# A LoRA kernel on one core: the first two stores are released by seven turned tiles of the fourth group

## The chip, the cores and the metric

The kernel runs on one core of one Trainium2 chip. The metric is the device time of one execution in microseconds (us). The kernel before was run three times: 123.61 us median, 123.61 to 123.78. The profile is of one execution that took 123.76 us by the same clock; its span, from the first instruction to the last, is 121.9 us, and 1.8 us lie around the span. The engines are TensorE (PE, with its weight loads as PEld), VectorE (DVE), ScalarE (ACT), GpSimd (POOL) and SyncE (SP), which here only issues transfers. The transfers are carried by the core's 16 DMA engines.

## The reference

```python
def setup_inputs():
    batch, seq, d_model, r = 16, 512, 768, 16
    return {
        "x": np.random.randn(batch, seq, d_model).astype(np.float32),
        "A": np.random.randn(d_model, r).astype(np.float32) * 0.1,
        "B": np.random.randn(r, d_model).astype(np.float32) * 0.1,
        "scale": 0.5,
    }

def reference(x, A, B, scale):
    lora = np.matmul(np.matmul(x, A), B)
    return (x + scale * lora).astype(np.float32)
```

x has 8192 rows of 768 float32 numbers, 25.2 MB. It is read once and a result of the same size is written once. A and B are 48 KB each. The arithmetic is one thin product with A (768 to 16), one with B (16 to 768) and an addition.

## The kernel before

**Tiles and groups.** A tile is 128 rows of x. The 64 tiles form eight groups of 8 (`GROUP`), numbered 0 to 7 in the code, so that the "fourth group" is group 3. All of x passes through one buffer in SBUF, `x_all`, with room for 48 tiles; the last 16 tiles use the place of the first 16 again. The result is added into the same place and stored from there. Row p of a partition holds neighbouring rows of x, so one partition's share of a transfer is one piece of 6, 18, 24 or 48 KB: such a piece is one DMA packet, each DMA engine carries the pieces of 8 of the 128 partitions, and after its 8 pieces of a transfer it writes 4 bytes that count as its part of the transfer's completion.

**One group's way.** ScalarE and GpSimd each cast 4 of the 8 tiles to half precision (`narrowed`, L186 to L196, into `xn`). VectorE turns the 8 tiles in blocks of 32 by 32 (`turned`, L248 to L250, `xn` to `xt`), viewed as 32-bit words, so that one tile is 384 elements a partition. TensorE multiplies with A in 24 matmuls (`projected`, L278 to L291). ScalarE scales the result into `y_bd` with four instructions (L238). TensorE multiplies with B, two tiles at a time (`raised`, L293 to L310): p from 0 to 3 is the pair, and each pair ends with an increment of `s_lora`. VectorE adds each pair to x (`summed(g, p)`, L252 to L259).

**Order on VectorE.** The loop at L265 to L271 is: for group g, wait for the product with A of group g (`s_y`, L267) and for both casts of group g+1 (`s_narrow`, L268), turn group g+1 in one instruction (L269), then add the four pairs of group g. So the fourth group is turned at g = 2, between the additions of group 1 and those of group 2.

**Order on TensorE.** In the loop at L324: pairs 0 and 1 of a group, then the wait for the next group's turn (`s_turned`), half of its product with A, pairs 2 and 3, the other half.

**Order on SyncE.** This engine issues all transfers, in the order in which they stand, and a wait holds back all that stands behind it:

- loads 0 to 5, which are tiles 0 to 47 (load 5 is the 16 tiles of groups 4 and 5, 6144 KB), without a wait among loads 2 to 5 (L160);
- `summed(0)` and `summed(1)`: wait until groups 0 and 1 are added;
- the wait of the change, L169: `s_lora` at 2 * 4 + 2 = 10, that is, TensorE has finished pairs 0 and 1 of group 2;
- store 0 (group 0) and store 1 (group 1), 3072 KB each;
- wait until store 0 is complete, then load 6 (group 6, in the place of group 0); wait until store 1 is complete, then load 7 (group 7);
- `summed(2)`, then the wait on `s_raise` at 6 (L181: TensorE has begun pair 0 of group 5), then store 2 (groups 2 and 3, 6144 KB);
- stores 3 and 4 (6144 KB each), each when VectorE has added its groups.

The loads and stores named here are those of the lists `LOADS` (L106) and `STORES` (L128).

Of the kernel before, what the change touches and what calls it, by code (L numbers as in the profile page):

```python
# [16 lines left out]
GROUP = 8  # L17
# [11 lines left out]
def kernel(  # L29
# [20 lines left out]
    PAIRS = GROUP // 2  # L50
# [32 lines left out]
    def sem(name):  # L83
        sems.append(nc.alloc_semaphore(name))
        return sems[-1]
# [10 lines left out]
    def memory(t2, i, s, n):  # L96
        S = PARTS[i]
        return t2[ds(parts[i], S * P), :].rearrange("(p s) d -> p s d", s=S)[:, ds(s, n), :]

    def held(i, s, n):  # L100
        return tiles(where.index((i, s)), n)

    def tiles(t, n):
        return x_all[:, ds(t % ROOM, n), :]
# [14 lines left out]
    s_first, s_narrow, s_turned, s_taken = sem("s_first"), sem("s_narrow"), sem("s_turned"), sem("s_taken")  # L119
    s_y, s_spread, s_lora = sem("s_y"), sem("s_spread"), sem("s_lora")  # L120

    s_free = [sem(f"s_free{p}") for p in range(PAIRS)]
    s_out0, s_out1, s_raise = sem("s_out0"), sem("s_out1"), sem("s_raise")

    s_sum, s_out = sem("s_sum"), sem("s_out")

# [8 lines left out]
    def on_sync(e):  # L135
        def load(k):
            ld = LOADS[k]
            e.dma_start(out=held(*ld), in_=memory(x2, *ld)).then_inc(s_load[k], 16)  # L138

        def summed(k):  # L140
            e.wait_ge(s_sum, k + 1)
            if STORED[k] + 1 < NG:

                e.sem_inc(s_free[PAIRS - 1], 1)

        def store(k, done):
            st = STORES[k]
            e.dma_start(out=memory(out2, *st), in_=held(*st)).then_inc(done, 16)

        load(0)  # L150
        load(1)
        e.wait_ge(s_ready, 1)
        blocks = A.rearrange("(c e) r -> c (e r)", e=64)
        for c in range(SETS):
            e.dma_start(
                out=a_rows[c : SET * SET : SET, :], in_=blocks[ds(c * SET, SET), :]
            ).then_inc(s_a, 16)
        e.wait_ge(s_brows, 1)
        e.dma_start(out=b_rows[0 : R * APART : APART, :], in_=B).then_inc(s_b, 16)
        for k in range(2, len(LOADS) - 2):  # L160
            load(k)

        for p in range(2, PAIRS):
            e.sem_inc(s_free[p], 1)
        summed(0)
        summed(1)


        e.wait_ge(s_lora, 2 * PAIRS + 2)  # L169
        store(0, s_out0)  # L170
        store(1, s_out1)
        e.wait_ge(s_out0, 16)
        load(len(LOADS) - 2)
        e.wait_ge(s_out1, 16)
        load(len(LOADS) - 1)
        for k in range(2, len(STORES)):
            summed(k)
            if k == 2:


                e.wait_ge(s_raise, 6)  # L181
            store(k, s_out)
# [58 lines left out]
    def on_vector(e):  # L241
        e.wait_ge(s_a, SETS * 16 + 1)
        e.transpose(  # L243
            out=a_t[0:Q].rearrange("i k r c -> i (k r) c"),
            in_=a_rows[0:Q].rearrange("c (i k r) -> c (k r) i", k=2, r=R),
        ).then_inc(s_ready, 1)

        def turned(first, n):  # L248
            ts = [v[:, ds(first, n), :].bitcast(fp32) for v in (xt, xn)]
            return e.transpose(out=ts[0], in_=ts[1])  # L250

        def summed(g, p):  # L252
            xs = tiles(g * GROUP + 2 * p, 2)
            e.wait_ge(s_lora, g * PAIRS + p + 1)
            ins = e.tensor_tensor(out=xs, in0=xs, in1=lora[p % 2], op=mybir.AluOpType.add)  # L255
            if p + 1 == PAIRS and g in STORED:
                ins.then_inc(s_sum, 1)
            elif g + 1 < NG or p + 2 < PAIRS:
                ins.then_inc(s_free[p], 1)  # L259

        for h in range(2):
            e.wait_ge(s_first, h + 1)
            ins = turned(h * SUB, SUB)
        ins.then_inc(s_turned, 1)
        for g in range(NG):  # L265
            if g + 1 < NG:
                e.wait_ge(s_y, g + 1)  # L267
                e.wait_ge(s_narrow, 2 * (g + 1))  # L268
                turned(0, GROUP).then_inc(s_turned, 1)  # L269
            for p in range(PAIRS):  # L270
                summed(g, p)  # L271

    def on_tensor(e):
# [58 lines left out]
        for p in range(PAIRS):  # L332
            raised(p)

    on_sync(nc.sync)
    on_gpsimd(nc.gpsimd)
    on_scalar(nc.scalar)
    on_vector(nc.vector)
    on_tensor(nc.tensor)

# [43 lines left out]
```

## Time and profile before

| what | value |
|---|---|
| median of three runs | 123.61 us (123.61 to 123.78) |
| profiled execution | 123.76 us, span 121.9 us |
| DMA queue, share of 16 engines over the span | 96.8%, 50.43 MB |
| DVE busy | 81.7 us (67%) |
| PE busy | 50.5 us (41%) |
| ACT busy, POOL busy | 37.4 us, 28.4 us |
| stores 0 and 1 issued from | 43.92 us |
| load 6 issued | 55.30 us |
| load 7 issued | 62.70 us |
| store 2 issued | 74.87 us |
| store 4 issued | 101.04 us |

All points in time are counted from the start of the span. A chain of waits names, for each stretch, the work that the next step waited for; a stretch that is called DMA runs from the issue of a transfer to its completion, so it holds both the time in which the transfer waits behind others and the time in which its bytes move. The trace also keeps, for each DMA packet, its start, its duration and its size; the 4-byte packets mark the moment at which one DMA engine has finished its part of one transfer.

### The profile page before, as it was taken

Reading aid. Unit: us, or ns where it says so; the run is one execution under the profiler, and the core shown is the slowest. Engines: PE = TensorE matmul, PEld = TensorE weight load, DVE = VectorE, ACT = ScalarE, POOL = GpSimd, SP = SyncE. Lnnn points to the kernel's source line nnn. Section 1 sums busy time; section 2 is a strip of 40 time slices with the busy share of each in tenths; the row PEclk is TensorE's granted clock in tenths of the full one; section 3 lists DMA queues with packets and bytes.
Section 4 is the critical chain, followed back from the end, with each engine's and each line's share of the span. In section 5 each row is a group of like instructions: output and inputs, shape, how many; then the busy total and the mean of one; then the engine's idle time right before and its main releaser. Section 6 shows DMA issues by size and latency. Waiting matters only on the chain.

```text
span 121.9 us, 885 instructions
## 1 busy us (share of the span) xinstructions
PE 50.5 (41%) x322; PEld 29.3 (24%) x322; DVE 81.7 (67%) x42; ACT 37.4 (31%) x43; POOL 28.4 (23%) x24
## 2 busy tenths in 40 slices
PE   0000239487457457647756714774674320000000
PEld 0000026244233233424424402442442110000000
DVE  0003850799999999999999959999995991000000
ACT  4003929444426402917230093643004000000000
POOL 7732638044026002607100090630000000000000
PEclk9999999999999999999999999999999985555555
DMA  3999999999997996999989999998998999899890
GB/s 67 421 429 429 443 443 403 451 435 419 476 516 339 435 516 298 460 403 443 443 363 460 427 427 468 451 484 387 419 500 387 403 516 403 371 516 419 355 516 0
DMA packets 1928, 50.43 MB, mean 414 GB/s; under 512 B 236, under 2 KB 236, under 8 KB 392
## 3 DMA queue, kind: packets, MB, share of 16 engines
q1 hardware_dynamic: 1928, 50.43, 96.8%
HBM read 25.26 MB, written 25.17 MB: 414 GB/s over the span
## 4 chain that ended last, share of the span: by engine, by line
DVE 33%; DMA 29%; PE 9%; ACT 6%; POOL 2%; issue 2%; SPq 0%; DVEq 0%
DVE x_sb L255 21%; DMA x_sb<-in_x_dram 20%; DVE xt L250 12%; DMA out_dram<-x_sb 9%; PE ps_yt L281 6%; ACT xn L194 3%; PE lora_ps L302 3%; ACT y_bd L238 2%; POOL xn L194 2%; SPq L138 0%; SPq L379 0%; DVEq L268 0%; SPq L133 0%
## 5 line engine op out<-in xcount | busy, mean ns | idle before, releaser
L255 DVE TENSOR_TENSOR x_sb<-x_sb,lora_ps 128x1536 f32<-128x1536 f32 x32 | 53.7, 1735 | 1.4 <-PE lora_ps L302 1.4
L302 PE MATMUL lora_ps<-b_mm,y_bd 128*128 128x512 f16 (+1 forms) x128 | 25.1, 328 | 23.7 <-ACT y_bd L238 15.3
L194 ACT CAST xn<-x_sb 128x3072 f16<-128x3072 f32 (+1 forms) x9 | 23.4, 2609 | 37.2 <-DMA x_sb<-in_x_dram 28.0
L250 DVE STREAM_TRANSPOSE xt<-xn 128x3072 f32<-128x3072 f32 (+1 forms) x9 | 27.0, 3005 | 6.7 <-PE ps_yt L281 4.9
L194 POOL CAST xn<-x_sb 128x3072 f16<-128x3072 f32 (+1 forms) x8 | 20.7, 2588 | 45.3 <-DMA x_sb<-in_x_dram 28.6
L281 PE MATMUL ps_yt<-xt,w_bd 128*128 128x256 f16 x192 | 25.7, 285 | 11.9 <-DVE xt L250 11.9
L281 PEld LDWEIGHTS ps_yt<-xt,w_bd 128*128 128x128 f16 x192 | 18.7, 100 | 19.6 <-issue 15.0
L302 PEld LDWEIGHTS lora_ps<-b_mm,y_bd 128*128 128x128 f16 x128 | 10.5, 97 | 36.8 <-ACT y_bd L238 17.5
L238 ACT ACTIVATE y_bd<-ps_yt 32x256 f16<-32x256 f32 x32 | 12.0, 374 | 17.7 <-PE ps_yt L281 17.4
L243 DVE STREAM_TRANSPOSE a_t<-a_rows 32x1024 f32<-32x1024 f32 x1 | 1.9, 1945 | 11.2 <-DMA a_rows<-in_A_dram 11.2
L315 PE MATMUL lora_ps<-b_half,pick 128*128 128x512 f16 (+1 forms) x2 | 0.8, 500 | 12.5 <-POOL b_half L212 12.5
L315 PEld LDWEIGHTS lora_ps<-b_half,pick 128*128 128x128 f16 x2 | 0.1, 105 | 12.5 <-issue 12.5
L220 POOL COPY w_bd<-w_one 32x384 f16<-32x384 f16 x4 | 2.0, 501 | 0.2
L212 POOL CAST b_half<-b_rows 128x768 f16<-128x768 f32 x1 | 0.8, 830 | 4.5 <-DMA b_rows<-in_B_dram 4.5
L194 ACT ACT_TABLE_LOAD x1 | 1.3, 1283 | 0.9 <-SPq L133 0.9
L202 POOL MEMSET w_bd<- 128x1536 f32 x1 | 1.4, 1372 | 0.0
L199 POOL MEMSET a_rows<- 32x1024 f32 x1 | 0.9, 941 | 0.5 <-SPq L133 0.5
L214 POOL CAST w_one<-a_t 32x384 f16<-32x384 f32 x1 | 0.8, 847 | 0.9 <-DVE a_t L243 0.9
L231 ACT CAST b_mm<-lora_ps 128x768 f16<-128x768 f32 x1 | 0.8, 798 | 0.0
L200 POOL MEMSET b_rows<- 128x768 f32 x1 | 0.7, 727 | 0.0
L203 POOL MEMSET y_bd<- 128x512 f32 x1 | 0.5, 514 | 0.0
L205 POOL TENSOR_SCALAR_AFFINE_SELECT pick<-pick 128x128 f16<-128x128 f16 x1 | 0.3, 300 | 0.0
(5 smaller groups left out, 0.6 us busy)
## 6 DMA issues: line engine op xcount, KB each, us to landing
out_dram<-x_sb SPq DMA_DIRECT2D x3, 6144.0 KB, 20.0
x_sb<-in_x_dram SPq DMA_DIRECT2D x5, 3072.0 KB, 14.8
x_sb<-in_x_dram SPq DMA_DIRECT2D x1, 6144.0 KB, 41.9
out_dram<-x_sb SPq DMA_DIRECT2D x2, 3072.0 KB, 14.9
x_sb<-in_x_dram SPq DMA_DIRECT2D x1, 2304.0 KB, 9.7
x_sb<-in_x_dram SPq DMA_DIRECT2D x1, 768.0 KB, 4.5
a_rows<-in_A_dram SPq DMA_DIRECT2D x3, 16.0 KB
b_rows<-in_B_dram SPq DMA_DIRECT2D x1, 48.0 KB, 7.4
```

The lines of the kernel that those rows point to most:

```text
L194: ins = copy(out=xn[:, ds(first, n), :], in_=tiles(t, n))
L199: e.memset(a_rows[0:Q], 0.0).then_inc(s_ready, 1)
L202: e.memset(w_bd.rearrange("p c k m -> p (c k m)").bitcast(fp32), 0.0)
L212: e.tensor_copy(out=b_half, in_=b_rows).then_inc(s_bh, 1)
L220: e.tensor_copy(out=w_bd[ds(b * Q, Q), :, :, ds(b * Q, R)], in_=w_one).then_inc(s_w, 1)
L238: last = e.mul(out=y_bd[q, :, q], in_=y_ps[q, :, :], mul=sc)
L243: e.transpose(out=a_t[0:Q].rearrange("i k r c -> i (k r) c"), in_=a_rows[0:Q].rearrange("c (i k r) -> c (k r) i", k=2, r=R),).then_inc(s_r ...
L250: return e.transpose(out=ts[0], in_=ts[1])
L255: ins = e.tensor_tensor(out=xs, in0=xs, in1=lora[p % 2], op=mybir.AluOpType.add)
L281: mm = e.matmul(y_ps, w_bd[:, c, k, :], xv[:, :, c, :, k], start=(m == 0), stop=(m == MMS - 1),)
L302: mms.append(e.matmul(t[:, k, ds(n0, w)], y_bd[:, 2 * p + k, :], b_mm[:, ds(n0, w)], start=True, stop=True,))
L315: last = e.matmul(lora[0][:, 0, ds(n0, w)], pick.rearrange("p b r -> p (b r)"), b_half[:, ds(n0, w)], start=True, stop=True,)
```

## The change

SyncE no longer waits for TensorE's tenth pair. It waits for a new semaphore, `s_most`, which VectorE raises when it has turned seven of the eight tiles of group 3. For that, the turn of group 3 becomes two instructions, one of 7 tiles and one of 1; the second carries the increment of `s_turned` for which TensorE waits. The other groups' turns stay one instruction of 8 tiles (the first group has two of 4, before and after).

```diff
@@ -121,6 +121,7 @@
     s_free = [sem(f"s_free{p}") for p in range(PAIRS)]
     s_out0, s_out1, s_raise = sem("s_out0"), sem("s_out1"), sem("s_raise")
+    s_most = sem("s_most")
@@ -166,7 +167,7 @@
         summed(1)
-        e.wait_ge(s_lora, 2 * PAIRS + 2)
+        e.wait_ge(s_most, 1)
         store(0, s_out0)
         store(1, s_out1)
         e.wait_ge(s_out0, 16)
@@ -266,7 +267,11 @@
             if g + 1 < NG:
                 e.wait_ge(s_y, g + 1)
                 e.wait_ge(s_narrow, 2 * (g + 1))
-                turned(0, GROUP).then_inc(s_turned, 1)
+                if g == 2:
+                    turned(0, GROUP - 1).then_inc(s_most, 1)
+                    turned(GROUP - 1, 1).then_inc(s_turned, 1)
+                else:
+                    turned(0, GROUP).then_inc(s_turned, 1)
             for p in range(PAIRS):
                 summed(g, p)
```

## The prediction

> **What bounds the kernel now.** I read the DMA part of the page first, then the shares by stage, then the chain of waits around the stores, and last VectorE's and SyncE's instructions in order of time.
>
> The page's queue line, and a table of stages with, after the clock, the DMA share and GB/s:
>
> ```profile
> q1 hardware_dynamic: 1928, 50.43, 96.8%
> ...
> 32.00:46.00 14.00, 8.08 (x54) 4.85 (x55) 14.00 (x7) 4.69 (x7) 2.75 (x1) 1.00 1.04 446
> 46.00:62.00 16.00, 9.76 (x68) 5.78 (x65) 16.00 (x10) 8.30 (x10) 5.50 (x2) 1.00 0.97 410
> 62.00:76.00 14.00, 7.60 (x48) 4.16 (x48) 12.69 (x6) 4.45 (x6) 2.75 (x1) 1.00 0.99 427
> 76.00:90.00 14.00, 8.64 (x59) 5.19 (x60) 14.00 (x9) 4.25 (x5) 2.75 (x1) 1.00 1.05 453
> ```
>
> A packet is booked in the stage where it starts, so a share can pass 1; what is to be seen is that no stage has a hole. The 16 engines move bytes from 2 us to the end: 50.43 MB in (120.6 - 2.0) us is 425 GB/s. The transfers are the bound, and compute matters only where it lets the queue run empty.
>
> The chain of waits seems to say otherwise, since it goes through the very instruction that is moved:
>
> ```profile
> 42.42 1.49 PE lora_ps L302 x8
> 43.91 0.02 issue
> 43.92 11.36 DMA out_dram<-x_sb
> 55.28 0.02 issue
> 55.30 14.76 DMA x_sb<-in_x_dram
> 70.06 0.05 issue
> 70.11 2.76 POOL xn L194
> ```
>
> Store 0 takes 11.36 us from issue to completion, but its 3.15 MB need 7.4 us at 427 GB/s. The other 4 us are waiting behind load 5. The packet records show this: the engines finish load 5 between 46.45 and 47.67, and on each the first packet of store 0 starts within 3 ns of that. Likewise load 6: 14.76 us, 7.4 of them behind store 1. So a transfer ends when the queue gets to it, and its issue may move as long as it still comes before its turn.
>
> **The change part by part.**
>
> ```profile
> 40.17 1.74 DVE L255 TENSOR_TENSOR x_sb<-x_sb,lora_ps 128x1536 f32<-128x1536 f32 x1
> 41.84 3.36 DVE L250 STREAM_TRANSPOSE xt<-xn 128x3072 f32<-128x3072 f32 x1
> 45.12 6.71 DVE L255 TENSOR_TENSOR x_sb<-x_sb,lora_ps 128x1536 f32<-128x1536 f32 x4
> ...
> 43.92 0.82 SPq L148 DMA_DIRECT2D out_dram<-x_sb  x2
> ...
> L250 DVE STREAM_TRANSPOSE xt<-xn 128x3072 f32<-128x3072 f32 x7 | 23.5, 3363 | 6.3 <-PE ps_yt L281 4.9 <-POOL xn L194 1.3
> L250 DVE STREAM_TRANSPOSE xt<-xn 128x1536 f32<-128x1536 f32 x2 | 3.5, 1751 | 0.4 <-ACT xn L194 0.4
> ```
>
> *When the stores go out.* A turn of 8 tiles takes 3363 ns, one of 4 takes 1751: (3363 - 1751) / 4 = 403 ns a tile and 1751 - 4 * 403 = 139 ns an instruction. Seven tiles: 139 + 7 * 403 = 2960 ns. The turn starts at 41.84, when the additions of group 1 leave VectorE; both casts of group 3 ended by 38.7. So `s_most` rises at 44.80 and SyncE issues at about 44.83 (it took 0.03 us after TensorE's pair before). That is 0.91 us **later** than 43.92, not earlier. The two earlier waits on SyncE, for groups 0 and 1, are met by 41.9 in both kernels.
>
> *What stands behind that wait.* On SyncE: stores 0 and 1, loads 6 and 7, and everything after. Store 1's issue moves to 45.25; its turn comes at 53.8. The first engine is free at 46.45, so store 0's lead shrinks from 2.52 to 1.62 us. Is that enough? The trace has two rows for the time from an issue to packets. Store 2 is issued at 74.87; the first engine leaves load 7 at 76.02 and goes on without a hole, so 1.15 us suffice. The first load, into an empty queue, is issued at 0.97; its first packet starts at 1.99 and the others' by 2.65, 1.0 to 1.7 us, with the start of the program in it. I take the nearer row, a transfer joining a running queue: 1.15 is under 1.62, cost 0. From the far row, the last engine could starve by 0.1 us.
>
> *Loads 6 and 7.* They are issued when stores 0 and 1 are complete (54.94 and 62.21 in the packets, 55.30 and 62.70 at SyncE), and their turns come at 61.5 and 68.7: leads of 6 us. Since the stores end when they did, these do not move. If store 0 did end later by up to 6 us, load 6 would still join the queue in time, but every byte behind a hole is late by the hole.
>
> *VectorE.* One more instruction. Alone it is 139 ns; the rows above show the next VectorE instruction starting 0.08 us before the last has ended (41.84 + 3.36 = 45.20 against 45.12), so the net is between 0.06 and 0.14 us; I take 0.10. TensorE's product with A of group 3, group 2's additions and all of groups 3 to 5 move by that. It ends here:
>
> ```profile
> 70.11 2.75 POOL L194 CAST xn<-x_sb 128x3072 f16<-128x3072 f32 x1 [11.66 <-DMA x_sb<-in_x_dram]
> 72.86 1.53 ACT L238 ACTIVATE y_bd<-ps_yt 32x256 f16<-32x256 f32 x4
> 72.97 3.38 DVE L250 STREAM_TRANSPOSE xt<-xn 128x3072 f32<-128x3072 f32 x1 [1.31 <-POOL xn L194]
> ```
>
> VectorE waits 1.31 us for the cast of load 6, which swallows the 0.10. Store 2 waits for ScalarE's scaling at 72.86, which stands behind ScalarE's own cast of load 6, so its lead of 1.15 us is untouched. Were the cover gone, 0.10 us would shorten that lead. Store 4 is issued at 101.04 and its turn comes at 105.0. So this costs 0. The Trainium skill, "VectorE: DVE Perf Modes", section on the TRN2 errata, gives a measured fixed term of about 150 cycles at 0.96 GHz per instruction, some 0.16 us, where this trace has 0.14; either is under 1.31.
>
> *The seam from load 5 to store 0.* One thing can still change. An undisturbed 48 KB packet takes 1.815 us. Of load 5's last ones, four (started 44.98 to 45.41) took 1.946, 1.880, 2.281 and 2.254: a mean of 0.065 us over the 16 engines. At the seam from store 1 to load 6 nine 24 KB packets took 1.1 to 1.7 us instead of 0.912: 0.27 us an engine. The seam from load 7 to store 2, whose store joined just 1.15 us ahead, has no stretched packet. No row shows what a lead of 1.62 us gives. Bounds: all stays (0), or the 0.065 goes and with it what follows. I take the nearer, at most 0.065 gained.
>
> **Sum.** Later stores 0, VectorE 0 (0.10 under 1.31), seam -0.065: the profiled 123.76 becomes 123.70. It lies 0.15 above the median of 123.61; carried over, **123.55 us**. A measurement of this kernel can tell about 0.2%, 0.25 us, from no change.
>
> **The rivals.**
>
> *Faster by the seam (0.32).* If stretched packets come from a store queued well ahead of its turn, the shorter lead removes them, and engines that leave load 5 within 0.8 us of one another (as they left load 4, 31.92 to 32.69) instead of 1.2 may also cross the next seam more cleanly. In full: 0.065 + 0.27 = 0.34 off the mean finish of 120.02, and the last engine 0.24 behind the mean instead of 0.54. The end moves from 120.56 to 119.92: 0.64 less, 123.0. Half of that: 123.3. For it: the clean seam at 76. Against it: the next seam's load has a lead of 6 us in either kernel.
>
> *Slower by a late store (0.13).* If the queue needs a lead over 1.62 us, each engine idles for the missing part and everything behind it is late: 0.25 us at a lead of 1.87; the full 0.91, 124.5, if a lead of 2.52 was just enough. For it: the chain of waits, and 1.7 us for the last engine of the first load. Against it: 1.15 us sufficed at store 2. The Trainium skill speaks for this side: "DMA: Bandwidth & Descriptors", in its rules for kernel authors, says to issue a DMA early so that its fixed cost overlaps. This trace bears that out only as far as the lead of 1.15 us.
>
> *Slower by a worse seam (0.11).* The stagger of the engines changes and the stretched packets fall on the last engine instead: one more of 0.45 us there gives 124.05. Nothing in the trace says which engine they hit.
>
> *That the change does not release as it says* is excluded: `s_most` rises once, and nothing else holds these stores after 41.9.
>
> **How the numbers follow.** No measurable change has 0.44, faster 0.32, slower 0.13 + 0.11 = 0.24. The likeliest alone: 123.4 to 123.8. The range takes in the seam's full gain at 123.0, and on the other side the worse seam and a late store by half its price: 123.0 to 124.15, with about 0.15 outside.
>
> **What would show it.** Stores 0 and 1 issued at 44.8 instead of 43.9; store 0's time to landing 10.4 instead of 11.4 us; load 6 still issued at 55.3; VectorE's wait for GpSimd's cast 1.2 instead of 1.3 us; turns of about 2960 and 540 ns. I am wrong if a DMA engine shows a hole near 46.5, if load 6 goes out later than 55.6, or if the seams near 46 and 61.5 look different.

## The result, and the profile after

The changed kernel took 124.15 us in the median of 7 runs (123.54 to 124.42), beside 123.71 us (123.46 to 123.96) for the kernel before. The ratio is 1.0039, with a 95% interval of 1.0022 to 1.0055: slower by about 0.44 us.

Inside the span nothing is slower. The profiled execution of the change took 124.27 us with a span of 121.9 us; the one before took 123.76 us with the same 121.9 us. The half microsecond lies around the span: 2.4 us instead of 1.8.

First the part that the prediction was about. The chain of waits of the changed kernel around the stores:

```profile
42.01 2.90 DVE xt L251
44.90 0.02 issue
44.92 10.45 DMA out_dram<-x_sb
55.37 0.02 issue
55.38 14.60 DMA x_sb<-in_x_dram
69.98 0.05 issue
70.04 2.76 POOL xn L195
```

The first two stores go out at 44.92 us, one microsecond later than before, and store 0 is complete when it was before, 55.37 against 55.28: its time to completion shrank by 0.9 us because it spends less time behind load 5. Load 6 starts and lands as before (70.06 before, 69.98 now).

The stages of the changed kernel, with clock, DMA share and GB/s at the end of each line, have no hole either:

```profile
32.00:46.00 14.00, 7.93 (x53) 4.72 (x54) 14.00 (x9) 4.79 (x7) 2.75 (x1) 1.00 1.04 451
46.00:62.00 16.00, 9.93 (x69) 5.92 (x67) 16.00 (x10) 8.15 (x10) 5.50 (x2) 1.00 0.97 415
62.00:76.00 14.00, 7.55 (x48) 4.16 (x48) 12.93 (x6) 4.62 (x6) 2.75 (x1) 1.00 1.00 428
76.00:90.00 14.00, 8.73 (x60) 5.25 (x61) 14.00 (x9) 4.26 (x5) 2.75 (x1) 1.00 1.03 446
```

VectorE's turns by shape, with their mean duration, and the idle time before them:

```profile
L251 DVE STREAM_TRANSPOSE xt<-xn 128x3072 f32<-128x3072 f32 x6 | 20.2, 3370 | 5.9 <-PE ps_yt L286 4.8 <-POOL xn L195 1.1
...
L251 DVE STREAM_TRANSPOSE xt<-xn 128x2688 f32<-128x2688 f32 x1 | 3.0, 2966 | 0.0
...
L251 DVE STREAM_TRANSPOSE xt<-xn 128x384 f32<-128x384 f32 x1 | 0.5, 541 | 0.0
```

The pieces take 2966 and 541 ns, and the wait for GpSimd's cast of load 6 shrinks from 1.3 to 1.1 us: the cover holds. In the packet records the end of store 4's last packet moves from 120.56 to 120.48 us.

What is new stands behind the span. This is the list of DMA queues of the changed kernel in the stretch from 120 to 126 us (kind of queue: packets, MB, share):

```profile
q14 instruction: 1, 0.01, 0.5%
q1 hardware_dynamic: 4, 0.00, 0.0%
```

and the same stretch of the kernel before:

```profile
q1 hardware_dynamic: 6, 0.00, 0.1%
```

The packet records put that one instruction packet at 124.00 us, 2.1 us after the last instruction of the span: 8192 bytes, 0.51 us long. By the kind of its queue it carries instructions, not data; for which engine, the records don't say. In the profiled execution of the kernel before, the last instruction packet stands 0.07 us ahead of the span. The last instruction of the span has ended by then; what an execution still does in its last two microseconds is not in the profile.

From here on, "time around the span" is a run's time less its span; each run lists both, the span to 0.1 us, so one such difference is good to 0.05 us. It is 1.94 to 2.54 us in the seven runs of the change, median 2.42; all 107 runs of the kernel before beside the experiments lie between 1.76 and 1.86, median 1.81.

### The profile page after: what moved, and what is told of

Its sections match the earlier page's. It is cut to its first block, busy times and chain, and to the rows that moved or that the text cites. A ratio compares the mean times of both kernels' runs of the same rounds, so it can differ in the third digit from the quotient of the medians.

```text
span 121.9 us, 886 instructions
## 1 busy us (share of the span) xinstructions
PE 50.3 (41%) x322; PEld 29.3 (24%) x322; DVE 81.8 (67%) x43; ACT 37.5 (31%) x43; POOL 28.4 (23%) x24
## 4 chain that ended last, share of the span: by engine, by line
DVE 38%; DMA 29%; PE 6%; ACT 5%; POOL 2%; issue 2%; SPq 0%; DVEq 0%
DVE x_sb L256 23%; DMA x_sb<-in_x_dram 20%; DVE xt L251 15%; DMA out_dram<-x_sb 9%; PE ps_yt L286 5%; ACT xn L195 3%; POOL xn L195 2%; PE lora_ps L307 1%; ACT y_bd L239 1%; SPq L139 0%; SPq L384 0%; DVEq L269 0%; SPq L134 0%
## 5 line engine op out<-in xcount | busy, mean ns | idle before, releaser
L251 DVE STREAM_TRANSPOSE xt<-xn 128x3072 f32<-128x3072 f32 (+3 forms) x10 | 27.2, 2723 | 6.1 <-PE ps_yt L286 4.8
```

## The experiments

Instructions are counted below in the built program, the list that the build makes of the kernel for each engine: 61 on VectorE before, 62 with the change.

Theory A: the added VectorE instruction lengthens that engine's program so that one more piece has to be fetched at the end. Theory B: the late stores cost something. Theory C: the added semaphore does, by one more to clear. Theory D: the cut turn itself does.

**Late stores alone.** No cut, no semaphore.

```diff
-        e.wait_ge(s_lora, 2 * PAIRS + 2)
+        e.wait_ge(s_taken, 4)
```

> The turn of group 3 stays one instruction and no semaphore is added; stores 0 and 1 wait for the second matmul of group 3's product with A (the semaphore s_taken at 4) instead of TensorE's tenth pair. They should be issued near 45.5 us, 1.6 us later than before and 0.7 later than in the change, 0.95 us ahead of their turn. If the loss of the change comes from late stores: slower than the kernel before by at least the 0.44 us of the change (124.15 or more). If the loss comes from what was added to the programs (one VectorE instruction, one semaphore): no loss, 123.7 within 0.2. The span before is 121.9, the rest 1.8 us; a lead under 1.15 us may also open a hole of up to 0.2 us in the queue, which then shows in the packets near 46.5.

Measured: 124.67 us against 123.59, ratio 1.008 (1.0067 to 1.0093). By its time alone that is the costly late store of the expectation. But this loss is inside the span, 122.9 us, and the time around it is 1.81 us. The stores went out not at 45.5 but at 46.38 us, since in this execution VectorE's turn started 0.6 us later and the semaphore came after TensorE's second matmul had ended. The chain of waits of this kernel:

```profile
45.97 0.40 PE ps_yt L281 x2
46.37 0.02 issue
46.38 8.72 DMA out_dram<-x_sb
55.11 0.02 issue
55.12 15.56 DMA x_sb<-in_x_dram
```

The engines left load 5 from 46.64 us on, 0.26 us after the issue, and the first packets of store 0 started at 47.24 to 47.38, 0.86 to 1.00 us after it. That is the time from an issue to its packets, and the queue stood empty for 0.27 us an engine. So a late store does cost when its lead is shorter than that time, about 1 us here; in the change it had 1.8 us in the profiled execution (issued 44.92, first engine free at 46.72). This run therefore doesn't test the change's own release. The larger part of this run's loss came later. Load 6 now takes 15.56 us from issue to landing instead of 14.76. With the engines restarted together, within 0.15 us of one another, they all met the step from store 1 to load 6 at the same moment, and 27 packets there were stretched, 0.80 us an engine against 0.27 before. That the common restart is the reason is read from this one profile and was not tested. The expectation named the hole in the queue, but neither the issue at 46.38 nor the loss at this step.

**The cut alone.** The turn of group 3 in 7 tiles and 1, the stores as before, no semaphore.

```diff
-                turned(0, GROUP).then_inc(s_turned, 1)
+                if g == 2:
+                    turned(0, GROUP - 1)
+                    turned(GROUP - 1, 1).then_inc(s_turned, 1)
+                else:
+                    turned(0, GROUP).then_inc(s_turned, 1)
```

> The turn of group 3 is two instructions, of 7 tiles and 1, and the stores wait for TensorE's tenth pair as before; no semaphore is added. If the added VectorE instruction costs outside the span: 124.1, with the span at 121.7 to 121.9 and 2.3 us or more around it. If late stores or the semaphore cost: 123.7, with 1.8 us around the span.

Measured: 124.23 us, ratio 1.0044 (1.0032 to 1.0057), the whole loss of the change without its late stores. Span 121.6 to 122.0; around it 1.91 to 2.50, median 2.38; an 8192-byte instruction packet at 123.97 us. B is out as the cause.

**The semaphore alone.** `s_most` is allocated and cleared, and nothing uses it.

> One semaphore more is allocated and cleared with the others; nothing waits for it. If the semaphore costs: 124.1. If the added instruction or the late stores cost: 123.7 within 0.2.

Measured: 123.68 us, ratio 1.0008 (0.9999 to 1.0018); 1.78 to 1.86 around the span. C is out.

**The cut in another group.** The condition of the cut is `g == 5`, the turn of group 6.

> The kernel before with the turn of group 6 as 7 tiles and 1, where the next work on VectorE is 0.1 us later and store 2 is already issued. If an added VectorE instruction costs wherever it stands: 124.1. If the place in group 3 matters (what it delays): 123.7.

Measured: 123.92 us, ratio 1.0027 (1.0015 to 1.0039). Around the span 1.87 to 2.42: three runs of seven near 1.9, four near 2.35. An instruction packet at 123.68 us. Its place in group 3 isn't what costs; that the time takes two values was not expected.

**The change with one VectorE instruction less elsewhere.** On top of the change, VectorE's own wait ahead of the turn of group 6 goes, because GpSimd's cast of that group now waits for the same event.

```diff
-                e.wait_ge(s_y, g + 1)
+                if g != 5:
+                    e.wait_ge(s_y, g + 1)
...
-            e.wait_ge(s_taken, g)
+            if first and g == 6:
+                e.wait_ge(s_y, g)
+            else:
+                e.wait_ge(s_taken, g)
```

> The change as it is (stores released by seven turned tiles, turn of group 3 in two instructions, the added semaphore), but VectorE's program is one instruction shorter elsewhere: its own wait for s_y ahead of the turn of group 6 is gone, because GpSimd's cast of that group waits for s_y instead of s_taken (one wait for another, GpSimd's count is the same). VectorE then has as many instructions as in the kernel before. That cast should start about 0.5 us later, within cover. If one VectorE instruction over some limit adds the half microsecond after the span: no 8192-byte instruction packet near 124 us, 1.8 us around the span, 123.6 (or down to 123.4 from the cleaner seam near 46). If the late stores or the split itself cost: 124.1 as in the change.

Measured: 123.70 us, ratio 1.001 (0.9996 to 1.0024); 1.76 to 1.85 around the span, no instruction packet. Late stores, cut and semaphore are all still there, and the loss is gone.

**The cut alone, with one VectorE instruction less.** The same edit on the cut alone.

> As the run before it, with the stores released as in the kernel before (TensorE's tenth pair) and no added semaphore. By the limit on VectorE's program: 123.6, no instruction packet after the span. By the split itself: 124.2, as with the split alone.

Measured: 123.54 us, ratio 0.9996 (0.9985 to 1.0008); 1.77 to 1.86 around the span. D is out: a cut turn at the old program length is free.

**Two instructions more.** The turn of group 3 as 6, 1 and 1: 63.

> The kernel before with the turn of group 3 in three instructions (6 tiles, 1 and 1): two VectorE instructions more than before. By a limit that is crossed once: 124.2, the same as with one more. By a price for each instruction: 124.8. By neither: 123.6.

Measured: 123.93 us, ratio 1.0025 (1.001 to 1.0039); around the span three runs at 1.8 and nine at 2.05 to 2.24. Less than with one more, so the price is neither per instruction nor fixed. The profiled execution is one of the three at 1.8, and it has no instruction packet behind the span.

**One more on ScalarE.** The last scaling of the last group in two halves.

```diff
+                if g + 1 == NG and b + 1 == NQ:
+                    e.mul(out=y_bd[q, 0:4, q], in_=y_ps[q, 0:4, :], mul=sc)
+                    last = e.mul(out=y_bd[q, 4:8, q], in_=y_ps[q, 4:8, :], mul=sc)
+                else:
+                    last = e.mul(out=y_bd[q, :, q], in_=y_ps[q, :, :], mul=sc)
```

> The kernel before with one more instruction on ScalarE: the very last scaling of the last group is done in two halves of 4 tiles each, about 0.3 us later at a place that leads store 4 by 4 us. ScalarE and VectorE both have 61 instructions in the built program before, TensorE 102, GpSimd 53, SyncE 41. If the limit lies at the 61st instruction of any engine's program: 124.1 and an instruction packet after the span. If it is VectorE's alone, or if VectorE's turn itself matters: 123.6.

Measured: 123.62 us, ratio 0.9997 (0.9985 to 1.0008); around the span 1.81 to 1.91, median 1.87, which is 0.06 more than before and lost in the rest. ScalarE had the same 61 instructions in the built program and has 62 here; a 62nd instruction does not cost the same on every engine.

**One less than before.** The edit of the two runs with one instruction less, on the kernel before: 60.

> The kernel before with VectorE's wait for s_y ahead of the turn of group 6 taken over by GpSimd's cast (one wait for another there): 60 instructions on VectorE instead of 61. It is the control for the same edit in the two runs with one instruction less, and looks for a gain under the limit. With a limit crossed once between 61 and 62: 123.6, 1.8 us around the span. If each instruction costs: 123.1.

Measured: 124.24 us, ratio 1.0064 (1.0048 to 1.0081); around the span 2.25 to 2.51, median 2.48. Both expectations fail: a *shorter* VectorE program costs as much as a longer one. A limit between 61 and 62 doesn't explain that. The two runs with this edit at 61 show that the edit itself is free, so what is left is the length; that it acts by where the program ends is an inference. No instruction packet behind the span is in this profile, although this execution had 2.25 us around the span.

**Four more.** The turns of groups 3 to 6 each as 7 and 1: 65.

> The kernel before with the turns of groups 3 to 6 each as 7 tiles and 1: four VectorE instructions more, 65. With 62 the time around the span was 2.4 us, with 63 it was 2.1, before 1.8. If the cost is that of a late fetch of the piece of program behind a boundary, it shrinks as more of the program stands behind the boundary, because the fetch is then asked for earlier: 1.8 to 2.0 us around the span, 123.6 to 123.8. If it is a fixed price of a longer program: 2.1 to 2.4 us, 123.9 to 124.2.

Measured: 123.99 us, ratio 1.0039 (1.0023 to 1.0055); around the span 2.17 to 2.25, an instruction packet at 123.74 us.

**Twelve more.** The turns of groups 4 and 5 as 5, 1, 1, 1 and that of group 6 as 2 and six times 1: 73.

> The kernel before with the turns of groups 4 and 5 in four instructions each and that of group 6 in seven: twelve VectorE instructions more, 73; up to 0.8 us more on VectorE behind the stores 0 and 1, in the cover of the wait for load 6 but for the last six, ahead of which store 2 is issued. By a late fetch: 1.8 us around the span, 123.6. By a fixed price: 2.1 to 2.4 us.

Measured: 123.92 us, ratio 1.0035 (1.0021 to 1.005), but now with 1.76 to 1.86 around the span. The packet stands inside the kernel now. The DMA queues of this execution between 80 and 90 us:

```profile
q1 hardware_dynamic: 88, 4.33, 100.2%
q14 instruction: 1, 0.01, 0.2%
```

It stands at 85.51 us, and the time around the span is that of the kernel before. But the store packet that starts 0.31 us after it, at 85.82, takes 2.266 us; a packet of this size takes 1.815 undisturbed. The median span is 122.1 us, 0.3 longer than before. The added turns or the packet can have done that; the run does not separate them.

**The change once more.**

> The change once more, beside the runs with 60, 65 and 73 VectorE instructions on the same chip: 62 instructions, so 2.4 us around the span and 124.1.

Measured: 123.77 us against 123.59, ratio 1.0019 (1.0003 to 1.0035). Around the span three runs of twelve at 2.34 to 2.48 and nine at 1.87 to 1.96. So the change costs either about 0.1 us or about 0.6 us in an execution; how often the larger one comes differed between the two comparisons (six runs of seven, then three of twelve), and why is open. The profiled execution is one of the three: 2.43 us, with an 8192-byte instruction packet at 124.05 us.

**One satisfied wait and no turn.** The kernel before with one more instruction of another kind, a wait whose condition already holds.

```diff
+            if g + 1 == NG:
+                for k in range(1):
+                    e.wait_ge(s_y, NG)
             for p in range(PAIRS):
                 summed(g, p)
```

> The kernel before with one more instruction on VectorE that is no turn: a wait for s_y at 8 ahead of the last group's additions, which was met long before the wait that follows it. 62 instructions on VectorE, no turn is split. If the count of VectorE's instructions decides: 1.9 to 2.4 us around the span and 123.7 to 124.1, with an 8192-byte instruction packet near 124 us. If the split turn decides: 1.81 us and 123.6.

Measured: 123.76 us, ratio 1.0012 (0.9998 to 1.0025); around the span eleven runs at 1.87 to 1.96 and one at 2.38, none at 1.81. These are the two values of the length 62 without any cut, though the larger one came only once: the values go with the count and not with the cut. The profiled execution is one of the eleven (1.88 us), and no instruction packet is in it.

**The change, padded.** The change plus 21 satisfied waits at the same place in the code; the build makes eleven instructions of them, so that VectorE has 73.

> The change as it is, with eleven more VectorE instructions, all of them satisfied waits for s_y ahead of the last group's additions: 73 instructions. If the length decides and 73 is harmless: an instruction packet inside the span instead of after it, 1.81 us around the span, 123.6, the same as the kernel before. If the split turn or the late stores cost: 124.1.

Measured: 123.80 us, ratio 1.0019 (1.0003 to 1.0034); 1.77 to 1.86 around the span. The DMA queues of this execution between 99 and 101 us:

```profile
q1 hardware_dynamic: 16, 0.79, 92.3%
q14 instruction: 1, 0.01, 1.0%
```

The packet stands at 99.96 us, and the store packet that starts at 100.27 takes 2.265 us instead of 1.815, as in the run with twelve more; no other profile has a store packet as long. The median span is 122.0 us, 0.2 longer than before: what is saved behind the span seems to be partly paid inside it.

**Together**, the time around the span by the number of VectorE instructions in the built program:

```
60   2.25 to 2.51              (6 runs)
61   1.76 to 1.86              (before, 107 runs; late stores; semaphore; both with one less)
61   1.81 to 1.91              (one more on ScalarE, 12 runs)
62   1.87 to 1.96 in 26 runs, 2.28 to 2.54 in 24 runs   (change twice, cut alone, cut of group 6, one wait)
63   1.78 to 1.81 in 3 runs, 2.05 to 2.24 in 9 runs
65   2.17 to 2.25              (7 runs)
73   1.76 to 1.86              (23 runs, the packet inside the span)
```

The packet goes with the larger times. Of the sixteen profiled executions, five have an instruction packet behind the span, and they are five of the six with more than 2.2 us around it: four at the length 62 (2.37 to 2.43 us) and the one at 65. The sixth is the one at 60, without a packet. The ten with less than 1.9 us, among them one at 62 and one at 63, have none.

The comparisons ran on several chips. The larger value at 62 came in ten runs of twelve and four of seven on one chip, in three of twelve on a second and in one of twelve on a third, with different programs; the runs do not separate the chip from the program.

## Why the prediction was wrong

**The step that failed** is the price of the added VectorE instruction: "the net is between 0.06 and 0.14 us", then swallowed by the 1.31 us of cover. Inside the span that is right; the step left out what the length of VectorE's program does outside the span, and gave no reason why that should be nothing. And the sum took the 1.8 us around the span for a constant: "the profiled 123.76 becomes 123.70". That term was 2.4 us in the first comparison. The cut alone shows the loss without the late stores, and the change with one VectorE instruction less shows it gone with everything else in place (1.76 to 1.85 us).

**Late stores, 0.** Right. The lead was 1.80 us, not the 1.62 of the prediction, because the first engine left load 5 at 46.72 instead of 46.45. The runs with the change's release and a harmless program length measure 1.001 (0.9996 to 1.0024) and, padded, 1.0019 with the packet inside the span. The late-store rival needed a lead over 1.62 us to be true; the run with late stores alone puts the need at 0.86 to 1.00 us, less than the 1.15 us that sufficed at store 2. In the profile of the change with one instruction less the lead was 1.17 us, and the queue has no hole.

**The forecast times.** 44.83 us for the issue was 44.92, because VectorE's additions ended 0.08 later; 2960 and 540 ns were 2966 and 541.

**The seam.** Its first half was right: no packet of load 5 was stretched in any of the five profiles with a lead of 1.8 us or less, and by and large the loss grows with the lead. From the packet records of six executions, lead of the issue over the first free engine, and mean stretch an engine of load 5's last packets:

```
change             1.80 us   0.00 us
two more           2.09 us   0.01 us
before             2.52 us   0.07 us
cut alone          2.74 us   0.11 us
semaphore alone    3.40 us   0.37 us
four more          3.38 us   0.54 us
```

The lead isn't all of it: one satisfied wait has 0.02 us at a lead of 2.48, twelve more 0.16 at 2.58.

That it would carry on to the next seam and gain up to 0.64 us was not: the stretch there was 0.06 us in the change's first profile and 0.29 in its second, and nothing in the semaphore run that had the 0.37. The stretch of the two seams together runs from 0.06 us (the change's first profile) to 0.55 (four more), and yet those two spans are 121.9 and 122.0, and the median spans of all kernels but the one with late stores alone lie within 121.7 to 122.1. Why is not shown.

**The direction.** The forecast was no measurable change, with 0.24 for slower. Both rivals for slower were about stores and seams, and neither was the cause. 124.15 us lies on the upper edge of the range, reached by another road. The second comparison has the change slower by 0.18 us (1.0003 to 1.0035), less than the 0.25 us from which the prediction would have spoken of a measurable change. So how far off the forecast looks hangs on how many executions took the larger value; the step that failed is the same in both.

**What stays open.** The packet shows that program is fetched behind the span at the lengths 62 and 65, and inside it at 73. Why 61 escapes between 60 and 62, why 62 has two values, and why the two kernels of length 73 fetch at 85.5 and 99.96 us, is not shown; at 60 no packet was recorded, and at 63 the profiled execution was a short one. That the fetch is what the end waits for is an inference from the two going together, not a measurement of that wait, and one figure speaks against its plainest form. In the change's profile the packet lands at 124.51 us, counted from the start of the span, but the whole execution took 124.27 us. The other three profiles of length 62 with a packet show the same within 0.01 us; at 65 it lands 0.17 us ahead. Unless the measured time began after the span did, the end did not wait for that packet to land.

The Trainium skill, "Runtime: NRT & Kernel Launch", section on instruction fetch mechanics, says that an engine's program is refilled in blocks and that crossing a boundary is mostly hidden. The traces agree for a fetch inside the kernel as far as the time around the span goes (1.76 to 1.86 us at 73), though a store packet beside it took 0.45 us longer. They differ for one behind it, where the profiled executions of length 62 that show it have 2.37 to 2.43 us around the span instead of 1.81.

## What to carry to other kernels

In a kernel whose transfers fill the whole span, a transfer may be issued at any time that leaves it its lead (0.86 to 1.00 us was needed here, and 1.17 us was enough), and moving the issue ahead of that gained nothing that these runs can tell. Compare time and span of every run before looking for a small loss inside the span: here the spans were equal and the whole difference lay outside. An instruction added to one engine can cost half a microsecond by the length that engine's program then has, so an edit of this size should be tried at a second program length before its idea is judged.

## What the runs showed of the hardware that was not expected

- The length of VectorE's program moves the time around the span between 1.8 and 2.5 us, and not in one direction: 60 and 62 instructions cost more than 61, 73 no more than 61.
- Taking one wait from VectorE (GpSimd waits in its place) made the kernel 0.64% slower (0.48 to 0.81), with the span unchanged.
- An 8192-byte instruction packet behind the span took 0.34 to 0.51 us in the profiles that show one. Inside the span, each of the two was followed 0.31 us later by a store packet of 2.27 us instead of 1.815.
- In one profile the DMA engines restarted within 0.15 us of one another after an empty queue, met the next step from stores to loads together and lost 0.80 us each there, three times the 0.27 us for which the queue had stood empty.
